# Parking the residual stream in device memory while two feed-forward layers run their first products, and four more seven-product tiles in the room it leaves

## The chip, the cores and the metric

The kernel runs on one core of a Trainium2 chip. The metric is device time in microseconds (us) of one execution; several runs are taken and the median is compared. The core has five instruction streams that are named here as the profile names them: PE (TensorE, matrix products), DVE (VectorE, elementwise work), ACT (ScalarE, elementwise and table functions), POOL (GpSimd) and SP (which here only issues transfers). Each works through its own instructions strictly in the order in which they stand, and waits on semaphores for the others. Transfers between device memory and the core's on-chip memory run on 16 DMA engines that all queues share. In the profile the transfers that SP issues are queue q1 ("hardware_dynamic") and those that POOL issues are queue q0 ("software_dynamic").

## The reference, cut to what matters

One residual block on 512 frames of width 1024, all in float32:

```python
def swiglu(h, w1, w3, w2):
    return (jax.nn.silu(h @ w1) * (h @ w3)) @ w2      # w1, w3: 1024 x 2816, w2: 2816 x 1024

x = x + 0.5 * swiglu(rms_norm(x, ffn1_norm), ffn1_w1, ffn1_w3, ffn1_w2)
h = rms_norm(x, mix_norm)
...                                  # two token mixers (a recurrence and an attention), gated and merged
x = x + (gate_a * y_a + gate_b * y_b) @ w_out
x = x + 0.5 * swiglu(rms_norm(x, ffn2_norm), ffn2_w1, ffn2_w3, ffn2_w2)
return rms_norm(x, final_norm)
```

The change sits in the two feed-forward layers (FFN1 and FFN2), and there in the first products, `h @ w1` and `h @ w3`.

## The kernel before

**Layout.** The stream `x` is held transposed: eight tiles `xT[0..7]` of 128 features by 512 frames (256 KB each), made at the start from the loaded rows `xin` by transposes on PE (`xtp`, line 273) and copied out of PE's accumulators by ACT (line 276). FFN1 adds its result into the same eight tiles. The mixers need the room, so FFN1's end saves them to device memory (`xsave`, line 792, issued by POOL), and they come back as `xS` (line 1418) before the output projection; FFN2 adds into those.

**Precision.** Each operand of a product is split in a high and a low part (`hi`, `lo`), and a product is three matrix instructions (`mm3`, line 133). A weight block is loaded raw (`load_raw`, 512 KB, line 110, issued by SP), cast by ACT to its high part (`whi`), and DVE makes the low part (`wlo`).

**First products.** The 2816 hidden features are 22 tiles `j` of 128. A plain tile makes `pa` (from w1) and `pb` (from w3), each with 8 blocks of 128 input features by 3 instructions of 512 columns: 48 instructions. A seven-product tile (class `Seven`, kind "S") does the same two products with Strassen's scheme in Winograd's form: seven products `z` of half-width operands, 7 x 4 x 3 = 84 instructions of 256 columns. It needs sums of weight blocks (`wsum`, by DVE, line 495), whose splits are `wtwo`, `wone` and a pair of `whi`/`wlo`, and sums of the activations, `E1` to `E4` (`e00h` ... `e31l`): 16 tiles of 256 KB, made once per layer by `Seven.sums`. Which tiles are of which kind stands in the call: FFN1 has `"fast": (5, 6, 8, 9, 11, 12, 14)` in the run from tile 4 to 14, FFN2 `(2, 3, 5, 6, 8, 9, 11, 12, 14, 15)` in the run from 1 to 15, so the pattern is two seven-product tiles and one plain one. Within the run the order of all instructions is written out by hand (`run`, with a list of steps after each product); elsewhere a scheduler, which simulates the program at build time, sets the order on each engine.

**Where the activation sums live.** Each hidden tile ends as a pair `hh{j}`, `hl{j}` (high and low part), and all 22 pairs must be kept for the second product (`pd`, with w2). The sums borrow places that a pair will need later:

```python
s.tags = [f"e{j}" for j in range(2 * own)] + [f"h{i}{j}" for j in range(KF - 8 + own, KF) for i in "hl"]
```

With `own` = 1 in FFN1, two places are the sums' own and fourteen are those of pairs 15 to 21; so no seven-product tile can come after 14. FFN2 has `own` = 2 and ends at tile 15.

**Raw buffers.** There are three buffers for raw weight blocks. A seven-product tile uses both blocks of the next tile while it runs: the weight sums are made from them.

**Second products.** `pd` for each of 8 output tiles m: 22 blocks by 3 instructions. DVE then scales and adds into `xT[m]` (lines 766 and 767).

Of the kernel before, what the change touches and what calls it, by code (L numbers as in the profile page):

```python
# [9 lines left out]
F32 = mybir.dt.float32  # L10
F32R = mybir.dt.float32r
# [7 lines left out]
P = 128  # L19
T = 512  # L20
D = 1024
KD = D // P
# [29 lines left out]
def kernel(  # L52
# [6 lines left out]
    nc = tc.nc  # L59
    dve, act, pool, pe = nc.vector, nc.scalar, nc.gpsimd, nc.tensor  # L60
# [3 lines left out]
    wp = ctx.enter_context(tc.tile_pool(name="wp", bufs=2))  # L64
# [4 lines left out]
    dp = ctx.enter_context(tc.tile_pool(name="dp", bufs=1, space=DRAM))  # L69
# [35 lines left out]

    def load_raw(aps, kt, n, raw=None, keep=False):
        if raw is None:
            raw = wp.tile([P, kt, n], F32, tag="raw", name="raw", bufs=3)
        for c0, src in aps:
            got = nc.sync.dma_start(raw[:, :, c0:c0 + src.shape[1]],  # L110
                                    src.rearrange("(k p) c -> p k c", p=P))
            if keep:
                tc.keep_in_program_order(got)
        return raw
# [26 lines left out]
        tc.keep_in_program_order(act.activation(out, in_, AF.Ln, **kw))  # L141


    def halved(src):
        hi, lo = tmp("shi", dt=F32R), tmp("slo", dt=F32R)
        act.copy(hi[:], src)
        dve.tensor_tensor(lo[:], src, hi[:].bitcast(F32), op=ALU.subtract)
        return hi, lo

# [19 lines left out]

    xctx = ExitStack()  # L170
    rtp = xctx.enter_context(tc.tile_pool(name="xr1", bufs=1, side="right"))
    xT = [rtp.tile([P, T], F32, name=f"xT{c}") for c in range(KD)]

    class Norm:


        def __init__(s, gain):
            s.hi, s.lo, s.gain, s.n = [None] * KD, [None] * KD, gain, 0
            s.acc = None
            s.rstd = None  # L180
# [54 lines left out]
            return mms  # L235

    par = cp.tile([P, PAR_N], F32, name="par")

    def pc(i):
        return par[:, i:i + 1]  # L240
# [10 lines left out]
    nrm = Norm(PAR_FFN1)  # L251
    with tc.tile_pool(name="x0", bufs=1) as x0:
        keep = tc.keep_in_program_order
        xin = [x0.tile([P, NB, D // 4], F32, name=f"xin{g}") for g in range(4)]
        own = [[x0.tile([P, 4, P], F32R, name=f"first{i}{w}") for i in "hl"] for w in range(4)]
# [11 lines left out]
        first = [bank(f"f{i}") for i in range(2)]  # L267
# [167 lines left out]
    class Seven:  # L435


        def __init__(s, nrm, w1, w3, hp, store, own, area, both, half, mid, out):
            s.nrm, s.w, s.hp, s.store = nrm, (w1, w3), hp, store
# [57 lines left out]
        def run(s, j, kind, nxt):  # L497
# [63 lines left out]
                    s.rest(new["p"][1][1][:], r[1][:], new["p"][1][0][:])  # L561

            a_, sa, h = tmp("fa"), tmp("fs"), tmp("fh")
            hi = s.hp.tile([P, T], F32R, name=f"hh{j}", tag=f"hh{j}")
            lo = s.hp.tile([P, T], F32R, name=f"hl{j}", tag=f"hl{j}")
            s.store(hi, lo)
            H = T // 2
            h0, h1 = slice(0, H), slice(H, T)
# [11 lines left out]
            if kind == "S":  # L580
# [17 lines left out]
                w3 = dv(W, Z[2], V, ALU.subtract)  # L598
# [78 lines left out]
    def ffn(nrm, w1, w3, w2, nxt, during=(), first=None, final=None, seven=None):  # L677
        with tc.tile_pool(name="hp", bufs=1) as hp:
            hh, hl, done = [], [], []

            def store(hi, lo):
                hh.append(hi)
                hl.append(lo)

            def evacuate():
                while done:
                    j, pa, pb = done.pop(0)
                    a = tmp("fa")
# [9 lines left out]
                    hi = hp.tile([P, T], F32R, name=f"hh{j}", tag=f"hh{j}")  # L698
                    lo = hp.tile([P, T], F32R, name=f"hl{j}", tag=f"hl{j}")
# [6 lines left out]
            sv = Seven(nrm, w1, w3, hp, store, seven["own"], *seven["places"](hp)) if seven else None  # L706
            for j in range(KF):
                c0 = j * P
                if sv and seven["from"] <= j < seven["to"]:
# [12 lines left out]
                else:  # L722
# [3 lines left out]
                    got = sv.ready.pop(j)["p"] if sv and j in sv.ready else (None, None)  # L726
# [22 lines left out]
                for n in range(2):  # L749
                    if sv and j == seven["sums"][n]:  # L750
                        with ExitStack() as order:
                            for i in sv.end if first else ():
                                order.enter_context(tc.issue_after(i.ins))
                            sv.sums(n)
            cuts = ((0, 8), (8, 8), (16, 6))

            for m in range(KD - (final is not None)):
                ps = bank("pd")
# [10 lines left out]
            if final is not None:  # L769
                m = KD - 1  # L770
# [24 lines left out]
    def early_places(hp):  # L795
        return (hp.tile([P, 4 * T], F32, name="wsum")[:], hp.tile([P, 4 * T], F32R, name="wtwo")[:],
                hp.tile([P, D], F32R, name="wone")[:], xp.tile([P, T], F32, name="mid", tag="acc", bufs=2)[:], tmp("gate")[:])

    ffn(nrm, ffn1_w1, ffn1_w3, ffn1_w2, mix_add, {2: load_params, 16: masks, 18: place_params}, first,
        seven={"fast": (5, 6, 8, 9, 11, 12, 14), "from": 4, "to": 15, "sums": (1, 2), "own": 1, "places": early_places, "after": None})  # L800

    W = w_in[0]

# [4 lines left out]
    with ExitStack() as mx:  # L808
# [236 lines left out]
        for t in range(C - 1):  # L1045
            n, m = t + 1, C - 1 - t
# [116 lines left out]
        for c in range(NC):  # L1163
# [11 lines left out]
            for p in range(NP):  # L1175
                h = half(p // 2)
# [47 lines left out]
        for p in range(NP):  # L1224
# [5 lines left out]
            for q in range(2):  # L1230
                h_, g_ = half(q), half(1 - q)
                h = 2 * p + q
# [59 lines left out]
        def proj_w(m, wt, own=None):  # L1292
            return load_w([(0, wt[0][:, m * P:(m + 1) * P])], NP, P, own=own, keep=wt is rwkv_proj or m > 3)
# [79 lines left out]
        fox(1)  # L1373
        squared(2)
        squared(3)
        fox(2)
        summing(0)
        summing(1)
# [37 lines left out]
        xT[:] = [rtp.tile([P, T], F32, name=f"xS{c}") for c in range(KD)]  # L1416
        for c in range(KD):
            nc.gpsimd.dma_start(xT[c][:], xsave[c])
        ms = []
# [53 lines left out]
    def final(h):  # L1473
# [45 lines left out]
```

## Time and profile before

| what | value |
|---|---|
| median of three runs | 1172.31 us (1171.69 to 1174.8) |
| the profiled execution's own time | 1172.94 us |
| its span in the trace | 1170.5 us (2.4 us of its time lie outside) |
| PE busy | 1155.1 us, 99% of the span |
| DVE, ACT, POOL busy | 768.9, 516.8 and 91.1 us |
| granted clock of PE | 0.999 of full speed |
| moved by DMA | 122.63 MB, mean 105 GB/s |

PE is busy nearly all the time, so what PE is given to do, and the few places where it waits, make the time. Times of single instructions in the trace overlap: a product of 512 columns is listed with 390 ns, but the next one starts 227 ns later. What a tile costs is therefore read from the starts of groups in the chain of waits and not from busy times.

### The profile page before, as it was taken

How to read it: one execution, taken by the hardware profiler on the slowest of the kernel's cores; microseconds unless marked ns; L12 is line 12 of the kernel's file. 1: busy time of each engine (PE TensorE's matmuls, PEld its weight loads, DVE VectorE, ACT ScalarE, POOL GpSimd, SP SyncE). 2: the span in 40 equal slices, each digit the busy share in tenths (PEclk: the TensorE clock that was granted, in tenths of full speed). 3: DMA queues.
4: the chain of work that ended last, by engine and by line, in shares of the span. 5: the costliest groups of instructions: out<-in, count | busy, mean ns of one | idle time of the engine just before them, and what ended most of it. 6: DMA issues, size and time to landing. Idle time of an engine off the chain costs nothing.

```text
span 1170.5 us, 17481 instructions
## 1 busy us (share of the span) xinstructions
PE 1155.1 (99%) x6954; PEld 970.7 (83%) x6954; DVE 768.9 (66%) x1214; ACT 516.8 (44%) x850; POOL 91.1 (8%) x141
## 2 busy tenths in 40 slices
PE   9999999999999999999999999999999999999997
PEld 7899998888887888887767777888999898888887
DVE  7988874444445888686756656879888885433342
ACT  6634432222224755246876657535444443222231
POOL 2000000000111112401000011121000000000000
PEclk9999999999999999999999999999999999999999
DMA  7333333334333343344112135533333334332331
GB/s 203 91 97 102 103 99 106 98 91 117 115 109 106 106 113 109 113 126 118 51 47 92 56 100 178 171 108 91 108 93 106 91 91 143 91 99 85 95 99 72
DMA packets 208191, 122.63 MB, mean 105 GB/s; under 512 B 9934, under 2 KB 200462, under 8 KB 208110
## 3 DMA queue, kind: packets, MB, share of 16 engines
q1 hardware_dynamic: 202110, 108.67, 32.1%
q0 software_dynamic: 3760, 12.06, 3.4%
q8 instruction: 54, 0.88, 0.3%
q10 hardware_dynamic: 2240, 0.79, 0.3%
q14 instruction: 27, 0.22, 0.1%
HBM read 110.82 MB, written 10.68 MB: 104 GB/s over the span
## 4 chain that ended last, share of the span: by engine, by line
PE 93%; DVE 4%; DMA 2%; ACT 1%; issue 1%; DVEq 0%; SPq 0%; ACTq 0%; POOLq 0%
PE pd L133 21%; PE z L133 13%; PE pa L133 12%; PE pb L133 12%; PE pgt L133 8%; PE pk L133 6%; PE pw L133 4%; PE pq L133 3%; PE ppj L1300 3%; PE pv L133 2%; PE pl L133 1%; PE lp L1280 1%; PE sps L1184 1%; DMA raw<-in_ffn_w_dram 1%; PE f L298 1%; PE gp L1002 1%
## 5 line engine op out<-in xcount | busy, mean ns | idle before, releaser
L124 ACT CAST whi<-raw 128x1024 fp32r<-128x1024 f32 (+2 forms) x141 | 139.0, 987 | 347.8 <-PE pd L133 154.2
L125 DVE TENSOR_TENSOR wlo<-raw,whi 128x1024 fp32r<-128x1024 f32 (+2 forms) x141 | 162.1, 1150 | 125.3 <-ACT whi L124 125.1
L133 PE MATMUL pd<-hh,wlo 128*128 128x512 f32 x330 | 128.9, 390 | 0.0
L133 PE MATMUL pd<-hl,whi 128*128 128x512 f32 x330 | 128.5, 389 | 0.0
L133 PE MATMUL pd<-hh,whi 128*128 128x512 f32 x330 | 128.4, 389 | 0.0
L133 PE MATMUL pa<-xl,whi 128*128 128x512 f32 x208 | 81.0, 390 | 0.0
L133 PE MATMUL pa<-xh,whi 128*128 128x512 f32 x208 | 81.0, 390 | 0.0
L133 PE MATMUL pa<-xh,wlo 128*128 128x512 f32 x208 | 81.0, 389 | 0.0
L133 PE MATMUL pb<-xh,wlo 128*128 128x512 f32 x208 | 80.9, 389 | 0.0
L133 PE MATMUL pb<-xh,whi 128*128 128x512 f32 x208 | 80.9, 389 | 0.0
L133 PE MATMUL pb<-xl,whi 128*128 128x512 f32 x208 | 80.9, 389 | 0.0
L133 PEld LDWEIGHTS pd<-hl,whi 128*128 128x128 f32 x330 | 61.9, 188 | 12.9
L133 PEld LDWEIGHTS pd<-hh,wlo 128*128 128x128 f32 x330 | 62.0, 188 | 12.8
L133 PEld LDWEIGHTS pd<-hh,whi 128*128 128x128 f32 x330 | 62.0, 188 | 12.6
L572 ACT ACTIVATE fs<-fa 128x512 f32<-128x512 f32 x26 | 16.4, 632 | 97.9 <-DVE fa L591 63.2
L133 PE MATMUL z<-xh,wlo 128*128 128x256 f32 x204 | 57.8, 283 | 0.6 <-DVE wlo L486 0.6
L133 PE MATMUL z<-xl,whi 128*128 128x256 f32 x204 | 57.7, 283 | 0.0
L133 PE MATMUL z<-xh,whi 128*128 128x256 f32 x204 | 57.7, 283 | 0.0
L133 PE MATMUL pgt<-xh,whi 128*128 128x512 f32 x128 | 53.4, 417 | 0.0
L486 DVE TENSOR_TENSOR wlo<-raw,whi 128x1024 fp32r<-128x1024 f32 x35 | 42.7, 1221 | 14.7 <-ACT whi L483 14.7
L483 ACT CAST whi<-raw 128x1024 fp32r<-128x1024 f32 x35 | 36.5, 1042 | 34.5 <-issue 33.7
L133 PE MATMUL pgt<-xl,whi 128*128 128x512 f32 x128 | 50.2, 392 | 0.0
(495 smaller groups left out, 2835.4 us busy)
## 6 DMA issues: line engine op xcount, KB each, us to landing
raw<-in_ffn_w_dram SPq DMA_DIRECT2D x116, 512.0 KB
raw<-in_w_in_dram SPq DMA_DIRECT2D x40, 512.0 KB
raw<-in_ffn_w_dram SPq DMA_DIRECT2D x15, 384.0 KB
raw<-in_w_out_dram SPq DMA_DIRECT2D x8, 512.0 KB
gsave<-gs SPq DMA_DIRECT2D x9, 256.0 KB
xin<-in_x_dram SPq DMA_DIRECT2D x4, 512.0 KB
xsave<-xT POOLq DMA_DIRECT2D x8, 256.0 KB, 2.5
G<-gsave POOLq DMA_DIRECT2D x8, 256.0 KB, 3.8
```

The source lines that it names most:

```text
L124: act.copy(hi[:], raw[:])
L125: (eng or dve).tensor_tensor(lo[:], raw[:], hi[:].bitcast(F32), op=ALU.subtract)
L133: mm = pe.matmul(ps, w, x_, start=first and n == 0, stop=last and n == 2)
L298: return keep(pe.matmul(first[w][:], wt, x_[:], start=k == 0 and n == 0, stop=k == KD - 1 and n == 2))
L483: keep(act.copy(dst, src))
L486: keep(dve.tensor_tensor(dst, src, f32(hi), op=ALU.subtract))
L572: keep(act.activation(sa[:], a_[:], AF.Silu))
L1002: gm = pe.matmul(gps[g][o, c], BK[s, cc], G[p][q][s, cc], start=True, stop=True)
L1184: hs = pe.matmul(sps[half(q), p, :], Dt[:, p, q, :], R[:, p, q, :], start=True, stop=True)
L1280: pe.matmul(av[half(q), j * P:(j + 1) * P], vt[k][:, h * 64:(h + 1) * 64], trs[q][:, o:o + P], start=k == 0, stop=k == b)
L1300: keep(pe.matmul(ps[:], a[:, k, :], y[k][b], start=k == 0 and n == 0, stop=k == NP - 1 and n == 2))
```

## The change

Five things are edited, and they hang together by the room they need.

1. `park()`: as soon as the activation sums exist, all eight `xT` tiles are written to device memory (`xpark`), by eight transfers of 256 KB issued by POOL. `unpark()`, after the last first-product tile in the program's text, allocates eight new tiles `xP` in the places `e0` to `e7` of the activation sums and reads them back, again by POOL. Both happen in FFN1 and in FFN2.
2. `place_h`: the pairs of tiles 10 to 13 now go into the eight places of the parked stream.
3. The room so gained holds more of the sums: `own` goes from 1 to 4 and from 2 to 5, so the sums borrow only from pairs 18 to 21 (19 to 21). The seven-product tiles then reach to 17 in FFN1 (15 and 17 are new) and to 18 in FFN2 (17 and 18 are new). `masks` and `place_params` move to tiles 19 and 20.
4. A fourth raw buffer.
5. In the recurrence's end, the casts of four weight blocks (`ahead_of`) are held until ACT has done the cast of the last square.

```diff
-            raw = wp.tile([P, kt, n], F32, tag="raw", name="raw", bufs=3)
+            raw = wp.tile([P, kt, n], F32, tag="raw", name="raw", bufs=4)
...
+    xpark = dp.tile([KD, P, T], F32, name="xpark")
...
-            hi = s.hp.tile([P, T], F32R, name=f"hh{j}", tag=f"hh{j}")
-            lo = s.hp.tile([P, T], F32R, name=f"hl{j}", tag=f"hl{j}")
+            hi, lo = s.place(j)
...
+            def place_h(j):
+                got = []
+                for i in "hl":
+                    n = 2 * (j - 10) + (i == "l")
+                    pool_, tag = (rtp, f"{seven['stream']}{n}") if 0 <= n < KD else (hp, f"h{i}{j}")
+                    got.append(pool_.tile([P, T], F32R, name=f"h{i}{j}", tag=tag))
+                return got
+
+            def park():
+                for c in range(KD):
+                    nc.gpsimd.dma_start(xpark[c], xT[c][:])
+
+            def unpark():
+                for c in range(KD):
+                    xT[c] = hp.tile([P, T], F32, name=f"xP{c}", tag=f"e{c}")
+                    nc.gpsimd.dma_start(xT[c][:], xpark[c])
...
+                if sv and j == seven["sums"][1]:
+                    park()
             cuts = ((0, 8), (8, 8), (16, 6))
+            if sv:
+                unpark()
...
-    ffn(nrm, ffn1_w1, ffn1_w3, ffn1_w2, mix_add, {2: load_params, 16: masks, 18: place_params}, first,
-        seven={"fast": (5, 6, 8, 9, 11, 12, 14), "from": 4, "to": 15, "sums": (1, 2), "own": 1, "places": early_places, "after": None})
+    ffn(nrm, ffn1_w1, ffn1_w3, ffn1_w2, mix_add, {2: load_params, 19: masks, 20: place_params}, first,
+        seven={"fast": (5, 6, 8, 9, 11, 12, 14, 15, 17), "from": 4, "to": 18, "sums": (1, 2), "own": 4, "stream": "xT", "places": early_places, "after": None})
...
         def ahead_of(m):
-            rw.append(proj_w(m, rwkv_proj, own=m))
+            with tc.issue_after(squares.ins):
+                rw.append(proj_w(m, rwkv_proj, own=m))
...
     ffn(nrm2, ffn2_w1, ffn2_w3, ffn2_w2, almost, final=final,
-        seven={"fast": (2, 3, 5, 6, 8, 9, 11, 12, 14, 15), "from": 1, "to": 16, "sums": (0, 0), "own": 2, "places": places, "after": after})
+        seven={"fast": (2, 3, 5, 6, 8, 9, 11, 12, 14, 15, 17, 18), "from": 1, "to": 19, "sums": (0, 0), "own": 5, "stream": "xS", "places": places, "after": after})
```

What the scheduler makes of it is seen in three places. The line numbers of the changed program are larger by up to 24.

First, POOL in the first microseconds. Before, its last preparation of masks (`sel`) is followed by the work on small parameters (`uw`, `ux`):

```order
L393 AFFINE_SELECT dmask<-dmask 128x128
L398 AFFINE_SELECT sel<-sel 8x8 x4
L427 CAST uw<-loraw 32x512
L428 CAST uw<-loraw 32x512
L430 CAST ux<-loraw 32x512
```

Now the eight parking transfers stand between them, right behind the masks:

```order
L401 AFFINE_SELECT sel<-sel 8x8 x4
L697 DMA xpark<-xT_111 128x512
L697 DMA xpark<-xT_112 128x512
L697 DMA xpark<-xT_113 128x512
L697 DMA xpark<-xT_114 128x512
L697 DMA xpark<-xT_115 128x512
L697 DMA xpark<-xT_116 128x512
L697 DMA xpark<-xT_117 128x512
L697 DMA xpark<-xT_118 128x512
L430 CAST uw<-loraw 32x512
L431 CAST uw<-loraw 32x512
```

The names `xT_111` to `xT_118` are the eight tiles of the stream. Each transfer waits for nothing but ACT's copy of its own `xT` tile; they do not wait for the activation sums, since reading a tile does not conflict with other readers. So they have moved to the very start of the program, ahead of `uw`.

Second, ACT at the end of FFN1's run. Before, tile 14 is the last seven-product tile, and the casts of plain tiles (line 124) follow:

```order
L483 CAST whi<-wsum 128x1024
L483 COPY fa<-z_1743 128x256
L483 CAST hh_1661<-fh 128x512
L483 CAST whi<-raw 128x1024
L572 ACTIVATE fs<-fa 128x512
L483 CAST whi<-raw 128x1024
L483 CAST hh_1741<-fh 128x512
L124 CAST whi<-raw 128x1024
```

Now the same eight places read so, with the sums of tile 15's weights cast during tile 14:

```order
L486 CAST whi<-wsum 128x1024
L486 COPY fa<-z_1752 128x256
L486 CAST hh_1670<-fh 128x512
L486 CAST whi<-raw 128x1024
L486 CAST wtwo<-wsum 128x1024
L486 CAST wone<-raw 128x512
L574 ACTIVATE fs<-fa 128x512
L486 CAST whi<-wsum 128x1024
```

The pattern of the run goes on for three more tiles. On PE the order of instructions is otherwise the same in the whole program but for a few places in the last output tile: two plain tiles of each layer have turned into 84 instructions of 256 columns each.

Third, POOL in FFN2. Before, the additions of the norm (`acc`) are followed by the load of the last norm's weights:

```order
L1418 DMA xS_6948<-xsave 128x512
L1418 DMA xS_6949<-xsave 128x512
L202 TENSOR_TENSOR acc<-acc,sq 128x512 x6
L1450 DMA fg<-in_final_norm_dram 128x1024
L1470 TENSOR_TENSOR facc<-facc,osq 128x512 x6
```

Now the eight reads from `xpark` stand ahead of that load; the last four of them and what follows:

```order
L702 DMA xP_9944<-xpark 128x512
L702 DMA xP_9942<-xpark 128x512
L702 DMA xP_9956<-xpark 128x512
L702 DMA xP_9954<-xpark 128x512
L1474 DMA fg<-in_final_norm_dram 128x1024
L1494 TENSOR_TENSOR facc<-facc,osq 128x512 x6
```

The reads wait for PE's last use of the places, and the load of the last norm's weights now waits behind them in POOL's order. The eight parking transfers of FFN2 are interleaved with the additions `acc`. On SP, the raw blocks that precede the load of the small parameters are four instead of three.

More of the change, by code (lines that the diff above doesn't have):

```diff
@@ L141, in ln_act @@
         tc.keep_in_program_order(act.activation(out, in_, AF.Ln, **kw))
+    marks = {}
     def halved(src):
         hi, lo = tmp("shi", dt=F32R), tmp("slo", dt=F32R)
-        act.copy(hi[:], src)
+        marks["cast"] = act.copy(hi[:], src)
         dve.tensor_tensor(lo[:], src, hi[:].bitcast(F32), op=ALU.subtract)
@@ L171 @@
     rtp = xctx.enter_context(tc.tile_pool(name="xr1", bufs=1, side="right"))
-    xT = [rtp.tile([P, T], F32, name=f"xT{c}") for c in range(KD)]
+    xT = [rtp.tile([P, T], F32, name=f"xT{c}", tag=f"xT{c}") for c in range(KD)]
     class Norm:
@@ L435, with __init__ @@
     class Seven:
-        def __init__(s, nrm, w1, w3, hp, store, own, area, both, half, mid, out):
-            s.nrm, s.w, s.hp, s.store = nrm, (w1, w3), hp, store
+        def __init__(s, nrm, w1, w3, hp, store, place, own, area, both, half, mid, out):
+            s.nrm, s.w, s.hp, s.store, s.place = nrm, (w1, w3), hp, store, place
             s.area, s.mid, s.out = area, mid, out
@@ L697, in evacuate @@
                     dve.tensor_tensor(h[:], b[:], sa[:], op=ALU.mult)
-                    hi = hp.tile([P, T], F32R, name=f"hh{j}", tag=f"hh{j}")
-                    lo = hp.tile([P, T], F32R, name=f"hl{j}", tag=f"hl{j}")
+                    hi, lo = place_h(j)
                     dve.tensor_copy(hi[:], h[:])
@@ L704, in evacuate @@
                         sv.end = [gate_, rest]
-            sv = Seven(nrm, w1, w3, hp, store, seven["own"], *seven["places"](hp)) if seven else None
+            sv = Seven(nrm, w1, w3, hp, store, place_h, seven["own"], *seven["places"](hp)) if seven else None
             for j in range(KF):
@@ L1375 @@
         squared(3)
+        squares = marks["cast"]
         fox(2)
@@ L1415 @@
         rtp = ctx.enter_context(tc.tile_pool(name="xr2", bufs=1, side="right"))
-        xT[:] = [rtp.tile([P, T], F32, name=f"xS{c}") for c in range(KD)]
+        xT[:] = [rtp.tile([P, T], F32, name=f"xS{c}", tag=f"xS{c}") for c in range(KD)]
         for c in range(KD):
```

## The prediction, made before the changed kernel was run

> **What bounds the kernel now.** I read the page first: the share of the engines, the granted clock, and the chain that ended last by engine.
>
> ```profile
> PE 1155.1 (99%) x6954; PEld 970.7 (83%) x6954; DVE 768.9 (66%) x1214; ACT 516.8 (44%) x850; POOL 91.1 (8%) x141
> PEclk9999999999999999999999999999999999999999
> PE 93%; DVE 4%; DMA 2%; ACT 1%; issue 1%; DVEq 0%; SPq 0%; ACTq 0%; POOLq 0%
> ```
>
> PE is busy at full clock from end to end, and 93% of the chain is PE. So a gain must come from giving PE less to do or from one of its few waits, and a loss must come as a new wait of PE. Next, the chain in order of time (start, length, what), at the first plain tiles of FFN1 and along FFN2's run:
>
> ```profile
> 22.62 5.44 PE pa L133 x24
> ...
> 61.21 5.44 PE pb L133 x24
> ...
> 826.17 20.15 PE z L133 x168
> 846.32 5.47 PE pa L133 x24
> 851.79 5.44 PE pb L133 x24
> 857.23 20.15 PE z L133 x168
> ...
> 888.29 17.29 PE z L133 x144
> ...
> 951.69 20.15 PE z L133 x168
> ```
>
> A plain tile is 5.44 + 5.44 = 10.88 us, two seven-product tiles are 20.15, so one is 10.08. The period of two seven-product tiles and a plain one is 857.23 - 826.17 = 31.06 us. From 888.29 to 951.69 are two periods, 63.40 us, where 62.12 were due: 1.28 us are lost there. The cause lies in the second of these periods: a piece of the chain there, the row of DVE's timeline that follows it (the idle time before an instruction stands in brackets), and what the queue of SP waits for (sum, count, longest):
>
> ```profile
> 920.34 5.66 DMA raw<-in_ffn_w_dram
> 926.09 0.69 DVE L495 TENSOR_TENSOR wsum<-raw 128x512 f32<-128x512 f32 x1 [1.28 <-DMA raw<-in_ffn_w_dram]
> SPq L110 <- DVE wsum L495: 142.5, 17, 11.5
> ```
>
> The raw block was issued at 920.3 and DVE went on at 926.1. It came late, since with three buffers SP may only issue it when DVE has finished with an earlier one; DVE's weight sums were late by 1.28 us, and PE's product with them.
>
> **The four tiles.** Each turns 10.88 us of PE into 10.08: 4 x 0.80 = 3.2 us. The first plain group after a seven-product pair takes 5.47 instead of 5.44, and there is one more such group in each layer: 0.06 back. Net -3.1 us. DVE and ACT get the work of the pattern that already runs at 31.06 us per period without a wait, in FFN2 five times. The new tiles continue this pattern, so I add nothing for them.
>
> **The fourth raw buffer.** Two raw blocks are in use by a seven-product tile and two can be in flight, so the next pair may be issued a whole tile (10 us) earlier than it is used. The wait of 1.28 us above goes: -1.3 us. If another transfer is just as late, 10 us cover it. The ends are 0 (it stays) and -1.3.
>
> **The return of the stream (`xP`).** Eight reads in each layer during tile 17 (18), right after PE's last use of the places. Their first use is the addition after `pd`'s first output tile, at the earliest three plain tiles (33 us) and 15 us of `pd` later. Nothing waits for them. But they take the DMA engines from the raw blocks; with the pair of the next tile already landed, and the pair after it wanted a tile later, I cost this at 0; the cover is the fourth buffer, and what it costs without that is a rival below. FFN2's load `fg` stands behind the reads and is wanted at the first `tokens`, 15 us into `pd`: 0.
>
> **The parking in FFN2.** One 256 KB transfer in each 5.4 us of the output projection, beside a raw block of 512 KB per 5.4 us. POOL is mostly idle there, each issue keeps it 0.55 us (row below), and the additions `acc` behind it wait for ACT's squares of the same tile anyway: 0.
>
> **The mixers.** PE's order is unchanged there, and so are those of DVE and ACT up to the recurrence's end. PE's longest wait in all of the program is small:
>
> ```profile
> PE ups L1177 <- DVE Xs L1173: 1.9, 2, 1.1
> ACT ownh L124 <- DMA raw<-in_rwkv_proj_dram: 3.5, 4, 1.5
> ```
>
> It does not come from a raw block. The second row is the wait of ACT in the casts of `ahead_of`, which now stand behind the squares: 0, with ends of -0.5 and +0.5, the sum of the short waits of PE around them (each 0.2, not more than the first row's longest).
>
> **The parking in FFN1** is the disputed cost. The order shows it at the very start of POOL, behind ACT's copies of `xT`. So these 2 MB start to move while the kernel's first loads are still landing. First the copies on ACT, then PE's transposes of the third and fourth quarter of the input:
>
> ```profile
> 6.21 0.59 ACT L276 COPY xT<-xtp 128x512 f32<-128x512 f32 x1 [3.46 <-PE xtp L273]
> 7.21 0.59 ACT L276 COPY xT<-xtp 128x512 f32<-128x512 f32 x1
> 9.13 1.08 ACT L276 COPY xT<-xtp 128x512 f32<-128x512 f32 x2 [0.58 <-PE xtp L273]
> 11.29 0.59 ACT L276 COPY xT<-xtp 128x512 f32<-128x512 f32 x1
> 12.27 0.59 ACT L276 COPY xT<-xtp 128x512 f32<-128x512 f32 x1 [0.39 <-PE xtp L273]
> ...
> 10.63 0.63 PE L273 MATMUL xtp<-ident,xin 128*128 128x128 f32 x4
> 13.15 1.04 PE L273 MATMUL xtp<-ident,xin 128*128 128x128 f32 x8
> 15.73 0.50 PE L298 MATMUL f<-xl,firsth 128*128 128x512 f32 x1 [0.15 <-DVE xl L283]
> ```
>
> Now what the queues move (packets, MB, share of 16 engines), in four stretches: from 0 to 9.25 us, from 0 to 11.42, from 9 to 10, and from 741 to 742 (POOL's transfers alone); then the two rows of one microsecond, 974 to 975, in which POOL's load `fg` and SP's raw block are both under way; and POOL's transfers in the page's list of issues (KB each, us from issue to landing) with the length of their issue:
>
> ```profile
> q1 hardware_dynamic: 2648, 2.11, 72.5%
> q1 hardware_dynamic: 3599, 2.84, 79.8%
> q1 hardware_dynamic: 357, 0.35, 109.1%
> q0 software_dynamic: 79, 0.26, 96.6%
> ...
> q0 software_dynamic: 89, 0.36, 87.1%
> q1 hardware_dynamic: 108, 0.06, 18.2%
> ...
> xsave<-xT POOLq DMA_DIRECT2D x8, 256.0 KB, 2.5
> fg<-in_final_norm_dram POOLq DMA_DIRECT2D x1, 512.0 KB, 5.1
> L792 POOL DMA_DIRECT2D xsave<-xT x8: 545/557/717, 263.0 to 368.6; - x8
> ```
>
> SP's queue is full from the start: it moves (2.84 - 2.11) / 2.17 us = 0.34 MB/us. The reader is to see the pair in the middle: when both queues have work, POOL's takes 0.36 MB in a microsecond and SP's 0.06. The packet counts, 89 and 108, are near to each other, but POOL's packets are 4 KB and SP's 0.5 KB. The packets of the input are 1 KB (0.35 MB / 357), so the input would get 108 / 89 x 1/4 of 0.36, about 0.1 MB/us, wherever a parking transfer streams.
>
> Working it through: by the order of issue the third quarter of the input (each 0.52 MB, with two weight blocks of 0.26 ahead) is in at 2.10 MB, the fourth between 2.62 and, if later packets mix in, 2.84 MB. A parking transfer streams for 1 us (0.26 MB) and lands 2.5 us after its issue, so it starts 1.5 us after its copy has ended. The copies end at 6.8, 7.8, 9.7, 10.2, 11.9 and 12.9; the transfers stream from 8.3 to 10.3, from 11.2 to 13.2 and from 13.4 to 15.4. SP's queue has 1.79 MB at 8.3, 1.99 at 10.3, 2.29 at 11.2 (the third quarter is in at 10.6, just in time), 2.49 at 13.2, 2.56 at 13.4; from there at 0.1 MB/us, 2.62 is reached at 14.0 and 2.84 at 15.6. PE wants it at 13.15 and stands in its order: 0.9 to 2.5 us late, and of that little is won back, since PE streams without a gap from 15.73 on. I take the middle, +1.7. The ends: 0, if a transfer that starts behind a full queue starts later (`fg`, behind a raw block, took 5.1 us where 1.5 + 2 = 3.5 were due; 1.6 us later start means the fourth quarter is in by 12.8), and 3.2, if POOL's packets pass with SP's fully held from 8.3 us on.
>
> A rule speaks for less. The Trainium skill (DMA: Bandwidth & Descriptors, "Queues, rings and completion order") says that each DMA engine takes turns between queues packet by packet, a packet being many descriptors; with packets of equal size each queue would get half. The trace agrees with turns (89 against 108) but not with equal bytes (0.36 against 0.06 MB). By the rule the sum would be that of the first rival's upper end.
>
> **The sum**, against the profiled execution's 1172.94 us (1170.5 of span and 2.4 around it): -3.1 (tiles) - 1.3 (raw wait) + 1.7 (start) = -2.7, so **1170.2 us**. The median of the runs, 1172.31, is 0.6 lower than this execution; the lowest, 1171.69, is near what it would be without the raw wait, so I leave the sum where it is. A measurement of this kernel can tell about 0.3% (3.5 us) from no change: below 1168.8 counts as faster, above 1175.8 as slower.
>
> **The rivals.**
> - *The start is free or nearly so.* If the two queues share bytes equally, SP's moves 0.17 instead of 0.34 MB/us beside a parking transfer: over the same stretches it has 1.79 MB at 8.3, 2.13 at 10.3, 2.44 at 11.2 and 2.78 at 13.2, so the fourth quarter (2.62 to 2.84 MB) is in between 12.3 and 13.4, at most 0.3 us late; with as much again for the weight blocks behind it, and nothing at all with late starts, the loss is 0 to 0.6, so 1168.5 to 1169.1 (1172.94 - 3.1 - 1.3 and the loss). For it: `fg`'s late start, and POOL shares its first microseconds with a full DVE. Against it: the row of 974 us. 30%.
> - *Slower, by the return of the stream.* Eight transfers stream for 6 to 8 us in tile 17 (18), and a raw block issued then gets 0.06 instead of 0.35 MB/us. If the pair for the next tile is issued only inside that burst, PE stands for most of it: some 5 us per layer, 10 in both, 1172.94 - 2.7 + 10 = 1180. It decides from about 3 us per layer on. Against it: the fourth buffer lets the pair go out a tile earlier. 7%.
> - *The raw wait stays or moves to another tile*: 1.3 us less gain, 1171.5. For it: the transfer's delay is not explained by the buffers alone (5.66 us from its issue at 920.34, against 1.5 us for 512 KB at 0.35 MB/us). 8%.
> - The forecast, a loss of 1 to 3 us at the start with the rest of the gain kept: 55%.
>
> **How the numbers follow.** The forecast's own range is 1168.9 to 1171.5. The range for 8 in 10 takes in most of the first rival and the third: 1168.2 to 1172.5. Faster by over 0.3%: most of the cheap half of the first rival (0.2) and an edge of the forecast (0.05), 0.25. Slower: the second rival with its smaller forms, 0.08. Within 0.3%: 0.67.
>
> **What the changed profile would show.** In the chain, 168 products `z` in 20.15 us at tiles 14/15 of both layers and 17/18 of FFN2, 84 in 10.08 at 17 of FFN1, and 31.06 us per period throughout FFN2: then the tiles and the fourth buffer are right. At the start, PE waiting for the transfer of `xin` before its last eight transposes, with the first plain `pa` starting at about 24.3 instead of 22.62 us: then the cost is right; if `pa` starts at 22.6, the first rival is. A wait of ACT or DVE for a raw block near tile 18 or 19, with PE idle behind it, is the second. I would be wrong altogether if the fourth buffer's new order of SP's queue delayed a transfer of the recurrence; PE would then show a wait between 545 and 720 us that it has not now.

## The result, and the profile after

The changed kernel takes 1167.5 us (median; 1167.29 to 1168.92), the kernel before, on the same chip, 1172.77 (1171.69 to 1174.8): a ratio of 0.9958, with an interval of 0.9943 to 0.9972. It is 5.3 us faster; 2.7 were forecast (from 1172.94 to 1170.2), and the range ended at 1168.2, 0.7 above the result. One of the twelve executions with three raw buffers (below) ran at a granted clock of 0.85 and took 1262.31 us; it is left out there.

The profiled execution took 1168.92 us, 1167.2 of them in the span. The page after, engines and chain:

```profile
PE 1152.9 (99%) x7098; PEld 975.8 (84%) x7098; DVE 790.1 (68%) x1260; ACT 526.7 (45%) x868; POOL 106.3 (9%) x173
PE 96%; DVE 3%; ACT 1%; issue 0%; DVEq 0%
```

The chain of the kernel before at places that were not shown yet (start, length, what), and then the chain after:

```profile
246.23 119.68 PE pd L133 x528
...
732.85 9.37 PE ppj L1300 x41
...
1037.15 20.86 PE pd L133 x92
1058.45 15.02 PE pd L133 x66
```

```profile
22.59 5.44 PE pa L133 x24
...
244.59 119.68 PE pd L133 x528
...
731.68 10.47 PE ppj L1322 x46
...
824.84 20.15 PE z L133 x168
...
949.08 20.15 PE z L133 x168
...
1033.21 20.96 PE pd L133 x92
1054.60 15.12 PE pd L133 x66
```

Subtract the starts of the same instructions or groups, after minus before, and the difference from place to place says where the time went (a minus means earlier than before):

| stretch | lead at its end | change in it | forecast |
|---|---|---|---|
| start, to the first `pa` | -0.03 | 0.0 | +1.7 |
| FFN1's tiles, to `pd` | -1.64 | -1.6 | -1.55 |
| recurrence, a stretch at half clock (below) | about -0.15 | +1.5 | not foreseen |
| recurrence's end, to `ppj` | -1.17 | -1.0 | 0 (±0.5) |
| output projection, to FFN2's first `z` | -1.33 | -0.2 | 0 |
| FFN2's run to tile 14 | -2.61 | -1.3 | -1.3 |
| tiles 17 and 18, to `pd` | -3.94 | -1.3 | -1.55 |
| FFN2's `pd`, to the end of the span | -3.3 | +0.64 | 0 |

The stretch at half clock is an accident of this execution: the two kernels with moved tiles (below), whose instructions stand in the same order, show none there. Columns here: length, busy time of PE, PEld, DVE, ACT and POOL with the instructions, granted clock, DMA share, GB/s; first after, then before:

```profile
603.50:607.50 4.00, 4.00 (x18) 2.52 (x14) 3.71 (x10) 2.08 (x5) 0.00 (x0) 0.57 0.00 0
```

```profile
603.50:607.50 4.00, 3.23 (x25) 2.27 (x24) 3.87 (x10) 2.65 (x7) 0.00 (x0) 1.00 0.00 0
```

The same products start 1.65 us earlier than before ahead of this stretch and 0.15 earlier behind it. Without the 1.5 us the profiled execution would stand at 1167.4, where three of the four other runs are (1167.29, 1167.48 and 1167.5; the fourth took 1168.68 at the lowest mean clock of the five, 0.996).

At the start, PE's last transposes begin at 13.15 as before. First POOL's first parking transfer, then what the queues had moved (packets, MB, share of 16 engines) from 0 to 10.3 us, from 10.4 to 13, and from 17 to 20:

```profile
7.10 0.72 POOL L697 DMA_DIRECT2D xpark<-xT  x1 [2.47 <-ACT xT L279]
...
q1 hardware_dynamic: 3327, 2.68, 84.6%
...
q1 hardware_dynamic: 890, 0.47, 60.4%
q0 software_dynamic: 136, 0.46, 48.4%
...
q0 software_dynamic: 276, 0.94, 79.4%
q1 hardware_dynamic: 470, 0.23, 27.3%
```

No row of q0 stands in the first answer: the transfer was issued at 7.10, and its first packet moved at 10.37. By 10.3 SP's queue had moved 2.68 MB. The input is the only load of this queue in packets of 1 KB, 2048 of them: 50 were left at 10.37, and the last moved by 11.5 us, as in the kernel before (11.4). While they moved, the two queues shared the bytes about equally (0.47 and 0.46 MB), and the input was in well ahead of 13.15. Only later does the forecast's picture hold: from 17 to 20 us POOL's queue gets four times what SP's gets, and the raw blocks come later. ACT's second cast of a raw block slips from 21.37 to 21.94, and PE does not see it.

### The profile page after: what moved, and what is told of

It is laid out like the page before. It is cut to its first block, busy times and chain, and to the rows that moved or that the text cites. A ratio compares the mean times of both kernels' runs of the same rounds, so it can differ in the third digit from the quotient of the medians.

```text
span 1167.2 us, 17947 instructions
## 1 busy us (share of the span) xinstructions
PE 1152.9 (99%) x7098; PEld 975.8 (84%) x7098; DVE 790.1 (68%) x1260; ACT 526.7 (45%) x868; POOL 106.3 (9%) x173
## 4 chain that ended last, share of the span: by engine, by line
PE 96%; DVE 3%; ACT 1%; issue 0%; DVEq 0%
PE pd L133 21%; PE z L133 18%; PE pa L133 10%; PE pb L133 10%; PE pgt L133 8%; PE pk L133 6%; PE ppj L1322 4%; PE pw L133 4%; PE pq L133 3%; PE pv L133 2%; PE pl L133 1%; PE sps L1206 1%; PE lp L1302 1%; PE f L301 1%; PE gp L1024 1%; PE lp L1291 1%
## 5 line engine op out<-in xcount | busy, mean ns | idle before, releaser
L124 ACT CAST whi<-raw 128x1024 fp32r<-128x1024 f32 (+2 forms) x129 | 126.4, 981 | 292.6 <-PE pd L133 147.9
L125 DVE TENSOR_TENSOR wlo<-raw,whi 128x1024 fp32r<-128x1024 f32 (+2 forms) x129 | 146.5, 1136 | 119.9 <-ACT whi L124 119.7
L133 PE MATMUL z<-xh,wlo 128*128 128x256 f32 x252 | 71.3, 283 | 0.0
L133 PE MATMUL z<-xl,whi 128*128 128x256 f32 x252 | 71.3, 283 | 0.0
L133 PE MATMUL z<-xh,whi 128*128 128x256 f32 x252 | 71.3, 283 | 0.0
L133 PE MATMUL pa<-xh,whi 128*128 128x512 f32 x176 | 68.6, 390 | 0.0
L133 PE MATMUL pa<-xl,whi 128*128 128x512 f32 x176 | 68.6, 390 | 0.0
L133 PE MATMUL pa<-xh,wlo 128*128 128x512 f32 x176 | 68.6, 390 | 0.0
L133 PE MATMUL pb<-xh,whi 128*128 128x512 f32 x176 | 68.5, 389 | 0.0
L133 PE MATMUL pb<-xh,wlo 128*128 128x512 f32 x176 | 68.5, 389 | 0.0
```

The costliest lines, as they stand in the source:

```text
L124: act.copy(hi[:], raw[:])
L125: (eng or dve).tensor_tensor(lo[:], raw[:], hi[:].bitcast(F32), op=ALU.subtract)
L133: mm = pe.matmul(ps, w, x_, start=first and n == 0, stop=last and n == 2)
```

## The experiments

**Parking later, first attempt.** The edit asks the builder to place the eight transfers behind the activation sums.

```diff
+ with tc.issue_after(sv.done.ins):      # sv.done: the last of the sums
      for c in range(KD):
          nc.gpsimd.dma_start(xpark[c], xT[c][:])
```

> The changed kernel with FFN1's eight parking transfers held until the activation sums are made (about 60 us), so that nothing but the loads moves at the start. Theory 1 (the parking costs nothing where it is, because its transfers start 3.3 us after their issue, when the input is nearly in): as the changed kernel, 1167.5, within 0.7; the first plain pa starts at 22.6 as before. Theory 2 (the parking costs the forecast 1.7 us somewhere, and another step gained that much more): 1165.8. In both, ACT's second cast of a raw block, which started at 21.94 instead of 21.37, goes back to 21.4.

Measured: 1168.6 us, ratio 0.9959 (0.9946 to 0.9973). It decides nothing: the edit sets an order in the builder's simulation but gives POOL no wait, POOL's order stayed as it was, and the first transfer was issued at 6.64 us. What it gives is a second execution of the same order: there the second quarter of the input was late (PE waited 0.87 us for it at 9.05, before the first parking packet at 10.65), and all that follows came 0.7 us later. So the start scatters by that much with nothing changed.

**Parking later, with a wait.** POOL now copies one column of the last sum first, and the transfers stand behind that.

```diff
+ held = pool.tensor_copy(late[:], sv.E[3][1][1][:, 0:1])
+ with tc.issue_after(held.ins):
      for c in range(KD):
          nc.gpsimd.dma_start(xpark[c], xT[c][:])
```

> The changed kernel with FFN1's eight parking transfers behind a small copy on POOL that reads the last activation sum, so that they are issued at about 60 to 70 us and not from 7 us on (the run before this one set only the builder's order, and POOL, with nothing else to do, still issued them at 6.6 us). Theory (late packets, free parking): the same time as the changed kernel, ratio to the kernel before 0.9958 within 0.001; ACT's first two casts of raw blocks at 19.0 and 21.4 us. Rival (1.7 us of cost are hidden in the changed kernel): ratio 0.9945 or less. A second rival: the parking then delays raw blocks of tiles 3 and 4, and PE shows a new wait between 60 and 100 us of 0.5 us or more.

Measured: 1168.04 us, ratio 0.9954 (0.994 to 0.9967), as with the changed kernel (0.9958). The interval still takes in the rival's 0.9945, so the medians alone do not decide; the traces do. With nothing parked at the start, the first `pa` begins 0.4 us later than in the changed kernel's execution and not 1.7 earlier; there is no new wait of PE between 60 and 100 us, and the raw casts at 19.4 and 21.75. The transfers:

```profile
56.90 4.55 POOL L701 DMA_DIRECT2D xpark<-xT  x8 [0.33 <-issue]
```

With SP's queue idle the first packet moves at 58.19, 1.29 us after the issue; at the start it was 3.27 in the changed kernel, and 3.4 to 4.4 in the ten other executions in which POOL parks there. So the lateness of the packets goes with a full queue of SP, and the parking cost nothing in the changed kernel's execution.

The margin is small. In the kernel without the hold (below), which parks in the same way, the last packet of the input moved at 13.45 us, 2 us later than in the changed kernel, and PE's last eight transposes show the very wait that the forecast had named:

```profile
14.30 1.06 PE L276 MATMUL xtp<-ident,xin 128*128 128x128 f32 x8 [0.44 <-DMA xin<-in_x_dram]
```

That execution's first `pa` is 1.2 us late, part of it from a wait for the second quarter, before any parking packet.

The kernel with the held parking also showed something that was not asked for:

```profile
245.04 120.53 PE pd L133 x528
...
825.26 19.98 PE z L133 x168
```

FFN1's second product takes 120.53 us instead of 119.68, and each pair of seven-product tiles of FFN2 19.98 instead of 20.15, with the same instructions. The one-column tile had moved most other tiles by 32 bytes (by the builder's addresses, which no trace shows); the last two experiments follow this up.

**A real backlog at the start.** Here the first two stream tiles are written four times.

```diff
- nc.gpsimd.dma_start(xpark[c], xT[c][:])
+ for i in range(4 if first and c < 2 else 1):
+     nc.gpsimd.dma_start(xpark[c + KD * i], xT[c][:])
```

> The changed kernel with the first two stream tiles written four times each (to places of their own), so that POOL's queue holds some 2 MB at once while the input and the first weights land. Theory (POOL's packets come late, but once they stream they take all but 0.08 MB/us from SP's queue): first parking packet again at about 10.4 us; then the last 0.13 to 0.35 MB of the input and the first weight blocks crawl, and the first plain pa starts 4 to 8 us late, at 26.5 to 30.5 instead of 22.6: 1171.5 to 1175.5. Rival (a parking transfer never holds up SP's loads much): pa at 22.6 to 23.5, 1167.5 to 1168.5.

Measured: 1172.26 us in one run, first packet at 10.36, first `pa` at 24.91 (22.42 in the changed kernel), 2.5 us late; the half clock that followed, from 26.2 to 29.6, and a second wait cost another 2.5. What the queues moved from 13 to 17 us, and PE's wait:

```profile
q0 software_dynamic: 431, 1.41, 87.0%
q1 hardware_dynamic: 430, 0.22, 18.0%
...
PE pa L133 <- ACT whi L124: 1.8, 1, 1.8
```

431 packets against 430: in these 4 us the two queues take turns packet by packet, and bytes go by packet size, 3.3 KB on average against 0.5 KB. The Trainium skill (DMA: Bandwidth & Descriptors, "Queues, rings and completion order") has the turns, and the trace agrees, though it does not tell whether a packet of the profile is one of the page's, which holds many descriptors. The equal bytes that the prediction drew from it for packets of equal size do not hold in these 4 us, since the packets are not equal. In the first 2.6 us, from 10.36 to 13, the bytes were about equal even here (0.45 MB from POOL, 0.51 from SP); why the share changes was not sought. The input again escaped: its last packet moved by 11.42. The weights did not. That `pa` was 2.5 us late and not 4 to 8 fits those first 2.6 us, in which SP's queue had 0.2 MB/us and not the 0.08 of the forecast. So the forecast's mechanism is real, but it set in later than forecast.

**The same transfers on ACT's queue.**

```diff
- nc.gpsimd.dma_start(xpark[c], xT[c][:])
+ (nc.scalar if first else nc.gpsimd).dma_start(xpark[c], xT[c][:])
```

> The changed kernel with FFN1's parking transfers issued by ACT, on a queue of their own, between its copies. Theory (a transfer's first packet waits behind what SP's queue has already handed to the DMA engines, whoever issues it): first packet of the first parking transfer 3 us or more after its issue, as on POOL's queue (7.10 to 10.37). Rival (POOL writes its descriptors late while DVE is busy): first packet 1 to 1.7 us after the issue, the fourth quarter of the input late, and PE standing 0.5 us or more before its transposes at 13.15.

Measured: 1179.61 us in one run. ACT issued its first transfer at 7.93, and the first packet moved at 11.55, 3.6 us later, so it is not POOL's way of writing descriptors that makes the first packet late. It fits a transfer that joins behind what SP's queue has already given to the engines. The loss, 11 us by the first `pa` (33.45), comes from elsewhere:

```profile
ACT xh L288 <- DMA raw<-in_ffn_w_dram: 4.6, 1, 4.6
ACT xT L279 <- DMA raw<-in_ffn_w_dram: 4.1, 1, 4.1
```

ACT waited ahead of an issue (a semaphore instruction stands before it) until a raw block had landed, and the copies of the input stood behind it. Why the issue waits for that block was not sought. Two stretches at half clock, at 17.9 and 24.7 us, each after a wait of PE, lie within the 11 us.

**Three raw buffers.**

```diff
- raw = wp.tile([P, kt, n], F32, tag="raw", name="raw", bufs=4)
+ raw = wp.tile([P, kt, n], F32, tag="raw", name="raw", bufs=3)
```

> The changed kernel with three raw buffers instead of four. If the fourth buffer is what removed both the 1.3 us of waits in FFN2's run and the 0.65 us at the recurrence's end (720 to 740 us), both come back: 1169.4 at the least, and 0 to 5 us more at tiles 17 to 19 of a layer, where the return of the stream shares the DMA engines with raw blocks that are then issued later: 1169.4 to 1174. If the gain at 720 us is due to the held casts and the wait in FFN2 moved by chance, 1167.5 to 1168.2.

Measured: 1172.42 us, ratio 0.9989 (0.998 to 0.9997): without the fourth buffer some three quarters of the gain are gone. By the starts in its trace, against the changed kernel's, 0.9 us is lost at the recurrence's end and 2.4 in FFN2's run, of which 1.35 at its first seven-product tile. DVE's waits in FFN2's run (sum, count, longest), with three buffers here and then in the kernel before; after the change this row does not exist:

```profile
DVE wsum L498 <- DMA raw<-in_ffn_w_dram: 4.8, 7, 2.1
```

```profile
DVE wsum L495 <- DMA raw<-in_ffn_w_dram: 2.3, 5, 1.3
```

So the buffer removes more than the 1.3 us that the trace before showed: with three of them the changed layout waits more than the old one did. Why the first tile suffers was not settled. At tiles 17 to 19 no wait for a raw block appears, with three buffers as with four, so the return of the stream is free. A small loss there has another cause: in the changed kernel the pair 17/18 of FFN2 takes 20.40 us instead of 20.15, since one weight load of PE waits 0.2 us for DVE's low part; with three buffers it takes 20.15. Why DVE is late there was not sought.

**The casts not held.** Four buffers, without the hold in the recurrence's end.

```diff
- with tc.issue_after(squares.ins):
-     rw.append(proj_w(m, rwkv_proj, own=m))
+ rw.append(proj_w(m, rwkv_proj, own=m))
```

> The changed kernel with the casts of ahead_of not held behind the squares. Theory (the 0.65 us at the recurrence's end come from the fourth raw buffer, which has the block there when ACT wants it): no wait of ACT for that block before the square's cast, PE's gain at 718 to 740 us kept within 0.2 us, 1167.5 within 1.5. Rival (the hold gives it): ACT waits about 1 us for the block as before, at about 719 us, and PE is 0.5 us later behind it.

Measured: 1170.61 us in one run (its first `pa` came 1.2 us late, as shown above). ACT's cast of the first held block, here, then in the kernel before, then after:

```profile
717.44 0.62 ACT L124 CAST ownh<-raw 128x512 fp32r<-128x512 f32 x1 [3.19 <-DMA raw<-in_rwkv_proj_dram]
```

```profile
720.37 0.62 ACT L124 CAST ownh<-raw 128x512 fp32r<-128x512 f32 x1 [1.04 <-DMA raw<-in_rwkv_proj_dram]
```

```profile
720.71 0.63 ACT L124 CAST ownh<-raw 128x512 fp32r<-128x512 f32 x1
```

Without the hold the cast stands ahead of a square's cast (`shi`), ACT waits 3.19 us for the block, and PE is 2.1 us later than in the changed kernel by 738 us. The rival was right, and more so than it said. With the run before this, all four combinations are there, in one trace each; PE at 738 us, against the kernel before (what had been won or lost up to 700 us taken out): hold alone -0.3, fourth buffer alone +1.1, both -1.0. Neither gives the gain by itself.

**The former lists of tiles.**

```diff
- "fast": (5, 6, 8, 9, 11, 12, 14, 15, 17)
+ "fast": (5, 6, 8, 9, 11, 12, 14)
- "fast": (2, 3, 5, 6, 8, 9, 11, 12, 14, 15, 17, 18)
+ "fast": (2, 3, 5, 6, 8, 9, 11, 12, 14, 15)
```

> The changed kernel with the former lists of seven-product tiles (none at 15 and 17 in FFN1, none at 17 and 18 in FFN2); parking, places, four raw buffers and held casts stay. Theory (four tiles at 0.80 us): 1167.5 + 3.1 = 1170.6. If the tiles gave less and the buffers and the order more, 1169 or lower; if the tiles gave all of it, 1172.5.

Measured: 1171.5 us, ratio 0.9985 (0.9976 to 0.9994). By the starts, FFN1 loses 1.6 us and FFN2 1.4: 3.0, where 3.1 were forecast.

**Three seven-product tiles in a row.**

```diff
- "fast": (5, 6, 8, 9, 11, 12, 14, 15, 17)
+ "fast": (5, 6, 7, 9, 10, 11, 13, 14, 15, 17)
- "fast": (2, 3, 5, 6, 8, 9, 11, 12, 14, 15, 17, 18)
+ "fast": (2, 3, 4, 6, 7, 8, 10, 11, 12, 14, 15, 16, 18)
```

> The changed kernel with three seven-product tiles in a row and then a plain one: ten instead of nine such tiles in FFN1, thirteen instead of twelve in FFN2. DVE is busy for 26.06 us of a period of 31.06, of which a plain tile takes some 4.2 us (two splits of 1.22 and 1.8 us of the tile's end) and so a seven-product tile some 10.9, against 10.08 of PE. Theory (DVE catches up in the plain tile): period 41.13 with 36.9 us of DVE, PE gains 0.8 us per layer: 1165.9. Rival (the third tile's sums are late by 0.8 us or more because DVE is slower than PE in a row): PE waits 0.8 to 2 us in each of the seven groups of three, 1168.5 to 1175.

Measured: 1173.95 us, ratio 1.0003 (0.9995 to 1.0012). DVE works almost without a pause through the second and third tile and needs 11.14 us from one to the next, as the same sum of weights in both shows, where PE needs 10.08:

```profile
874.83 0.69 DVE L498 TENSOR_TENSOR wsum<-raw 128x512 f32<-128x512 f32 x1
...
885.97 0.69 DVE L498 TENSOR_TENSOR wsum<-raw 128x512 f32<-128x512 f32 x1
```

A group of three and a plain tile takes 42.1 us instead of 41.1, and that is lost in each of seven groups.

**The same, with POOL taking two of DVE's operations; and all tiles seven-product.**

```diff
- hm = dv(h[:], b_[:], sa[:], ALU.mult)
+ def hm(): keep(pool.tensor_tensor(h[:], b_[:], sa[:], op=ALU.mult))
+ def hrest(): keep(pool.tensor_tensor(lo[:], h[:], f32(hi[:]), op=ALU.subtract))
```

> Three seven-product tiles in a row, and of each seven-product tile the last multiplication (hm) and the low part of its result (hrest), 0.6 us of DVE each, done by POOL, which is idle in these runs. The run before showed DVE turning round such a tile in 11.14 us where PE needs 10.08. Theory (DVE's work per tile is the bound): 11.14 - 1.2 = 9.9 us, less than PE's, so the waits of 0.9 to 1 us in each group of three go, and two more seven-product tiles than in the changed kernel give 1.6 us: 1167.5 - 1.6 = 1165.9, ratio to the kernel before 0.994. Rival (POOL's 1.9 us per such operation slow DVE, or come late for ACT's cast behind them): DVE's operations are longer beside POOL's, PE still waits in each group, ratio 0.996 to 1.003.

> As the run with it, but every tile from 5 to 17 of FFN1 and from 2 to 18 of FFN2 is of the seven-product kind: 13 instead of 9 and 17 instead of 12. Theory (DVE needs 9.9 us per tile, PE 10.08): nine tiles at 0.8 us are 7.2 us, 1160.3, ratio 0.989. Rival (DVE above 10.08 us per tile, with no plain tile to catch up in): the tile takes what DVE takes; at 10.9 us or more nothing is gained over plain tiles, ratio 0.996 to 1.01.

Measured: 1175.58 us (ratio 1.0016, 1.0007 to 1.0025) and 1192.82 (1.0166, 1.0152 to 1.018). Both rivals held, the second beyond the 1.01 that it said: a tile takes 11.1 us there, more than a plain one (10.88). A sum of weights on DVE, alone and beside POOL's subtraction (884 to 887 us of the first kernel):

```profile
876.03 0.69 DVE L498 TENSOR_TENSOR wsum<-wsum,raw 128x512 f32<-128x512 f32 x1
...
885.85 1.46 DVE L498 TENSOR_TENSOR wsum<-raw 128x512 f32<-128x512 f32 x1
```

DVE's sum takes 1.46 us instead of 0.69, and ACT's casts, which now wait for POOL's product, come later: in the first of the two kernels a tile turns round in 11.3 us. The plain tile in every three is what lets DVE and ACT catch up.

**Places in on-chip memory.** Two kernels whose instructions stand in the very order of the changed one, with some tiles moved:

```diff
+ ctx.enter_context(tc.tile_pool(name="pad", bufs=1, side="right")).tile([P, 48], F32, name="pad")
  rtp = ctx.enter_context(tc.tile_pool(name="xr2", bufs=1, side="right"))
```

> The changed kernel with 192 bytes of each partition left empty ahead of the FFN2 stream's tiles, so that they start at 1824 within a block of 2048 bytes, as all other hidden tiles do, and not at 2016 (before, all hidden tiles of both layers started at 1824); the order of all instructions is the same. It moves wtwo and wone of FFN2 too, from 1824 to 1632. In the changed kernel an output tile of FFN2's second product takes 15.12 us where it took 15.00 before, and in the kernel with the held parking, whose places are shifted by 32 bytes, a pair of seven-product tiles of FFN2 took 19.98 instead of 20.15 and FFN1's second product 120.53 instead of 119.68. Theory (PE's rate depends a little on where a product's two operands lie to each other): 15.00 us per output tile again, 0.8 us less in all, and perhaps 19.98 per pair, another 1.0: 1165.7 to 1166.7. Rival (the places have nothing to do with it): 15.12 and 20.15, 1167.5.

```diff
  rtp = ctx.enter_context(tc.tile_pool(name="xr2", bufs=1, side="right"))
+ rtp.tile([P, 8], F32, name="pad", tag="pad")
```

> The changed kernel with 32 bytes left empty behind the FFN2 stream's tiles: those stay at 2016, wtwo and wone of FFN2 go from 1824 to 1792 within a block of 2048 bytes; the order of all instructions is the same. Theory: a pair of seven-product tiles of FFN2 takes 19.98 us instead of 20.15 (six pairs, 1.0 us), an output tile of its second product stays at 15.12: 1166.5. Rival: 20.15 and 15.12, 1167.5.

Measured: 1167.15 us (ratio 0.9944, 0.993 to 0.9958) and 1167.48 (0.9947, 0.9933 to 0.9961). Pairs of FFN2 and an output tile of its second product, for the one and for the other:

```profile
824.43 20.03 PE z L133 x168
...
1053.40 15.02 PE pd L133 x66
```

```profile
823.14 19.98 PE z L133 x168
...
1052.03 15.12 PE pd L133 x66
```

The pitches came as the theory said; the medians did not (1165.7 to 1166.7 and 1166.5 were expected). The offsets are the builder's, and no trace shows them. With the hidden pairs 10 to 13 at the offset of the others (1824) an output tile takes 15.02 again; with `wtwo` and `wone` moved against the sums a pair takes 19.98 to 20.03. By the starts in their traces, from 610 us to the end, the first gains 1.2 us on the changed kernel (half clock apart) and the second 0.9; the medians do not tell the three apart.

## Why the prediction was wrong where it was

- **The parking in FFN1 (+1.7) is the step that failed.** Its "so it starts 1.5 us after its copy has ended" took the lateness from transfers that POOL made alone. Beside a full queue the first packet came 3.3 us after the issue, at 10.37 and not at 8.3, when 50 of the input's 2048 packets were left. That is the whole error of the term: from 10.37 and 2.70 MB on, the step's own 0.1 MB/us reaches 2.84 MB at 11.8, before PE wants the input at 13.15. The low end of its own bounds (a later start, as with `fg`) was the truth; the middle was taken without a reason. The rest of the step, who gets the engines once both queues have work, held only later: from 10.4 to 13 us SP's queue moved 0.18 MB/us, about as much as POOL's, and it fell to 0.08 MB/us only from 17 us on, and to 0.05 in the kernel with the backlog. The cost is not always zero: one execution shows 0.44 us of this wait.
- **The mixers (0, with ends of ±0.5) were mis-sized:** -1.0 us, and -0.2 in the output projection behind them. The row of ACT's wait for the raw block was quoted, 3.5 us in four waits, and priced by the short waits of PE next to it; what counts is that squares stood behind ACT's wait on the way to PE. Hold and buffer are needed together.
- **FFN2's second product was not priced:** +0.64 us, from the new offset of four hidden pairs.
- **The four tiles** (-3.1) measured -2.9 in the chain (0.25 of it lost in tile 18 of FFN2), -3.0 by the run without them. **The fourth buffer** in FFN2's run: -1.3, as forecast. **Return of the stream** and parking in FFN2: 0, as forecast.
- **The base of the sum,** 1172.94, held 2.4 us outside the span; in the kernel before this scatters from 1.7 to 3.3 us, and in the execution after it was 1.7. So 0.7 us of the miss is luck of the execution that was taken as base.

From 1172.94: -2.9 - 1.3 - 1.0 - 0.2 + 0.64 gives 1168.2, and with 0.7 less outside the span 1167.5, beside 1167.4 for the execution after without its half clock. The first rival, a free start (1168.5 to 1169.1), was right in its mechanism, in both its forms (equal bytes and a late start), and missed the recurrence's end. The raw wait did not stay, and the slower rival did not come: no wait for a raw block at tile 17, 18 or 19.

Three small readings of the prediction are off, and the sum does not use them. The longest single wait of PE is 1.2 us (`lp`, behind ACT's `qrn`), not 1.1. With SP's queue fully held from 8.3 us on, the step's own stretches reach 2.62 MB at 16.8 us, 3.6 us late and not 3.2. A loss of 1 to 3 us at the start is 1169.5 to 1171.5, not 1168.9 to 1171.5.

## What to carry to other kernels

Take a transfer's start latency from a row in which the other queue is as full as it will be, not from one where it runs alone, and when the bounds of a step hold two stories, choose between them by such a row. A wait of an engine that is not the bound is priced by what stands behind it in that engine's order; another buffer and a changed order can give little or lose when made alone, and gain together. When tiles change their places, compare the pitch of products whose instructions did not change.

## What the runs showed of the hardware

- A transfer that joins a full DMA system shows its first packet late: 3.3 to 4.4 us after its issue at the start (POOL's queue, eleven executions; 3.6 from ACT's), 2.5 us in a shorter burst (193.19 to 195.72, the return in FFN1), against 1.1 to 1.3 us when SP's queue moves nothing.
- Who gets the engines is not fixed: in the first 2.6 us the two queues moved about equal bytes (0.47 and 0.46 MB), and with a longer backlog about equal numbers of packets (430 and 431), and then POOL's larger packets take most of the bytes.
- PE's pitch depends on where operands lie, with the same instructions in the same order: 192 bytes of padding took an output tile of `pd` from 15.12 to 15.02 us and a pair of seven-product tiles from 20.15 to 20.03, 32 bytes elsewhere took the pair alone to 19.98, and a one-column tile took FFN1's `pd` from 119.68 to 120.53. This is under 1% of a stretch; the rule behind it was not sought.
- The granted clock fell to one half for 3.4 us at about 604 us (in slower kernels later, at the same place of the program) in seven of the fourteen profiled executions, the changed kernel's among them, costing 1.5 us in the two where it was compared by starts. In the 3.4 us ahead of it (600.40 to 603.80 in the changed kernel) PE was busy for 1.48 us, in waits of 1.17 and 0.77 us. The Trainium skill (TensorE: Matmul & The Clock Gate, "Part 1: The HAM clock gate (the "warmup" mystery)") gives half rate after an idle window of about 3.4 us on a free-running grid; the length agrees, but here a window that was 44% busy was enough. That the grid's phase decides which execution is hit fits this and was not tested.
